# Gate products in the other ring of result banks, norms' sums in the second tile behind, adaLN products out of the query tiles

## The chip, the core and the metric

The kernel runs on one core of one Trainium2 chip. The metric is the device time of one execution in microseconds, taken as the median of several runs. The kernel before takes 1669.76 us (three runs, 1668.8 to 1671.15). Its profile is one further execution.

Five engines work side by side, each through its own instructions in a fixed order, and they wait for each other by semaphores: TensorE (PE, matrix products), VectorE (DVE), ScalarE (ACT), GpSimd (POOL) and SyncE (SP, which issues the DMA loads). "Bank" below means one of the result banks that TensorE writes and that DVE and ACT read.

## The reference

One layer of a hybrid backbone on 256 latent tokens `x` and 256 context tokens `ctx`, width 2048. What matters here:

```python
sh1, sc1, g1, sh2, sc2, g2 = split(silu(c) @ w_ada + b_ada, 6)     # adaLN
h = rms_norm(x, norm1_w) * (1 + sc1) + sh1                         # and the same for ctx
gq, gk, gv, gr, gaf, gab, dq, dk, dv = split(h @ w_in, IN_OFFSETS)
la = log_sigmoid(ga @ w_a_up + b_a) / 16                           # gates of the linear attention
o  = gla_scan(gq, gk, gv, la)                                      # forward and backward, 8 heads
q, k = rope(rms_norm(dq)), rope(rms_norm(dk))                      # per head, width 64
od = (softmax(q0 k0) - lam * softmax(q1 k1)) @ dv                  # differential attention
mix = (sigmoid(..) * (ya @ w_proj_gla) + sigmoid(..) * (yb @ w_proj_diff)) @ w_out
x = x + g1 * mix;  x = x + g2 * conv_ffn(modulated(x))
```

Everything is float32 in and out. The products with weights are made of two rounded halves of each weight (a high half and a low half).

## The kernel before, in words

**Tiles.** Each weight product is a "tile": 128 output columns for all tokens. A tile's weights come in two loads of 512 KB (`fetch`, L233), each split into halves: ACT casts the high half (`whi`, L212), DVE subtracts it to get the low half (`wlo`, L219). Four raw buffers and three buffers of each half go round. The products read them: `col_tile` (L281, L283: latent tokens, lines for `gq`, `gr`, `dq` and the gates) makes 32 products of two lengths for a tile, `col_tile2` (L356 to L358: both streams, `gk`, `dk`) makes 48 long ones. `gv_chunk` and `dv_chunk` (L294 to L296) make value rows: a chunk holds four accumulating banks at once and takes eight loads with 24 products each.

**Stages.** After the first sweep come, in program order: two `gv` chunks, the key and query tiles of the linear attention, the `dk` tiles and `gr` tiles, with four calls of `gla_pair` among them (pairs 0 to 3, two heads each), then `dv_chunk(0)`, `dq` tiles 0 to 3, `dv_chunk(1)`, and eight heads of the differential attention between gate tiles; then projections, output product and feed-forward part, which the change does not touch. A scheduler with a time model of its own sets the order of each engine's instructions from the program's; the pairs and the attention heads have a higher priority, so their small products are put among those of the tiles.

**One `gla_pair`.** Two gate products `z` (L825), one for each direction, each into one bank. ACT and DVE make logarithms and running sums of them (`m`, `l`, `bfb`, `rc`). Then decay factors `e` for each of eight groups: POOL subtracts (`away`, L925), ACT takes exponentials (L928), DVE multiplies (`e`, L930). TensorE makes scores `sc` from the factors (L895) in three groups, of 16, 12 and 8 products with turned keys (`kT`) and states (L879) between; DVE's masked copies `at` (L938) empty the score banks. At the end come the outputs `o` (L959, L962) and their norm's sum `oss` (L701).

**Rings.** Banks are handed out in rings: `acc` with four, `aux0` with two and `aux1` with two. `aux_bank(name, j)` picks `aux0` or `aux1`. Score groups take pairs of one bank from each; turned keys, norm sums and `z` come from `aux0`; the outputs take one of each.

**Norms.** At the end of each `dk` and `dq` tile `heads_norm` copies the bank (`nraw`) and squares it (`nsq`) on ACT and puts a closure in the list `later`. That closure splits the squares into two halves (ACT and DVE, `nlo`, L238) and puts a second one in the list `latest`: the sums `hss` (two products, L660 and L661, in a bank of `acc`), the inverse root (ACT, L318 to L322, DVE), and the rotary part (`roped`: DVE shuffle L714, POOL multiplications L715 and L716, DVE sum L717). `flush` runs the closures of a list. The tiles call it halfway: `flush()` ahead of the second load, and `flush(latest)` some products later in the same half. All norm buffers of the `dk` tiles are single; the `dq` tiles use them as two halves in turn.

**adaLN products.** 128 pieces of the adaLN matrix (512 KB each) are multiplied with a broadcast row and summed on DVE (L380, `araw`). `ada_next(n)` adds `n` to a due count; for each whole piece that falls due it issues DVE's product on the older of two buffers (`ada_dot`) and then SP's load of the next into it (L374). The amounts stand at the tiles' calls and, for gate tiles, in `GATE_ADA`.

Of the kernel before, what the change touches and what calls it, by code (L numbers as in the profile page):

```python
# [45 lines left out]
LATE_ADA = {13: 1, 14: 2}  # L46
ROWS_AT = [4, 4, 2, 1]
WARM = 14
GATE_ADA = [0.25] * 4 + [0.5] * 16 + [1] * 12
NRM = [(0, 0)] * 2 + [(j, j + 1) for j in range(12)] + [(12, 14), (14, 16)]  # L50

_VEC = {}
# [100 lines left out]
def layer_kernel(tc, I, out):  # L153
# [3 lines left out]
    with es:  # L157
# [8 lines left out]
        def aux_bank(name, j=0):  # L166
            return ps.tile([P, 512], F32, tag=f"aux{j}", bufs=2, name=name)
# [33 lines left out]
        later, latest = [], []  # L201

        def flush(work=later):
            for step in [work.pop(0) for _ in range(len(work))]:
                step()
# [49 lines left out]
        def col_tile(src, acts, b, orders=None, adas=0):  # L255

            nk = src.shape[1]
            nq = nk // 4
            tied = orders is not None
            orders = orders or [TURN] * (nq - 1) + [ENDED]
            for k0 in range(0, nk, 8):
                kn = min(8, nk - k0)
                if k0:
                    flush()
                raw = fetch(src[:, k0:k0 + kn, :].rearrange("p a b -> p (a b)"), kn * P)
                if k0 and adas:  # L270
                    ada_next(adas)
                whi, wlo = split(raw[:, :kn * P], kn * P)
                for kk in range(0, kn, 4):
                    order = orders[(k0 + kk) // 4]
                    for which in order:
                        j = int(which[1])
                        k = k0 + kk + j
                        sl = slice((kk + j) * P, (kk + j + 1) * P)
                        first, last = k == 0 and which == "h0", k >= nk - 4 and which == order[-1]
                        if which[0] == "h":  # L280
                            i = PE.matmul(b.rearrange("p (a b) -> p a b", a=2), whi[:, sl], acts[k], start=first, stop=last)  # L281
                        else:
                            i = PE.matmul(b[:, T:], wlo[:, sl], acts[k][:, 1, :], start=False, stop=last)  # L283
                        if tied:
                            tie(i)
                    if k0 and not kk:
                        flush(latest)

        def added(dst, b):
            S.copy(dst, b[:, :T])  # L290
# [457 lines left out]
        with tc.tile_pool(name="gla", bufs=1) as pg:  # L748
# [34 lines left out]
            def col_tile2(src, b, adas=0):  # L783

                for k0 in range(0, KT, 8):
                    if k0:
                        flush()
                    raw = fetch(src[:, k0:k0 + 8, :].rearrange("p a b -> p (a b)"), 1024)
                    if k0 and adas:
                        ada_next(adas)  # L790
                    whi, wlo = split(raw, 1024)
                    for kk in range(8):
                        k = k0 + kk
                        both_tile(b, k, whi, wlo, slice(kk * P, (kk + 1) * P), k == 0, k == KT - 1)
                        if k0 and kk == 3:
                            flush(latest)

            def dk_tile(h):
                ada_next(0.5 if h > 3 else 0.75)
# [10 lines left out]
            def gla_pair(p):  # L810
# [9 lines left out]
                S.copy(wa, wr)  # L820
                V.tensor_tensor(wa[64:96], wr[64:96], wa[64:96].bitcast(F32), op=ALU.subtract)
                for d in range(2):
                    z = aux_bank("z")
                    bias = vcol("ba", d * 4 + p)
                    PE.matmul(z, wa[:, d, :], gaT, start=True, stop=True)  # L825
                    l = pg.tile([P, 512], F32, tag="l", name="l")
                    m = pg.tile([P, 512], F32, tag="m", name="m")

                    S.activation(m, z, AF.Relu, scale=-1.0, bias=nba[:, d * 4 + p:d * 4 + p + 1])
                    S.activation(l, z, AF.Abs, bias=bias)  # L830
                    S.activation(l, l, AF.Exp, scale=-1.0)
                    S.activation(l, l, AF.Ln, bias=1.0)
                    V.scalar_tensor_tensor(m, m, -1.0, l, op0=ALU.mult, op1=ALU.subtract)
                    V.memset(rc[:, d, (T - 1) * (1 - d):(T - 1) * (1 - d) + 1], 0.0)
                    if d == 0:
                        for c in range(2):
                            V.tensor_tensor_scan(bfb[:, 0, c * P:(c + 1) * P], onec[:, :P], m[:, c * P:(c + 1) * P],
                                                 0.0, op0=ALU.mult, op1=ALU.add)
                        V.tensor_tensor_scan(rc[:, 0, T - 2::-1], onec[:, :T - 1], m[:, 2 * T - 1:T:-1],
                                             0.0, op0=ALU.mult, op1=ALU.add)  # L840
                    else:
                        V.tensor_tensor_scan(bfb[:, 1, P - 1::-1], onec[:, :P], m[:, P - 1::-1],
                                             0.0, op0=ALU.mult, op1=ALU.add)
                        V.tensor_tensor_scan(bfb[:, 1, T - 1:P - 1:-1], onec[:, :P], m[:, T - 1:P - 1:-1],
                                             0.0, op0=ALU.mult, op1=ALU.add)
                        V.tensor_tensor_scan(rc[:, 1, 1:], onec[:, :T - 1], m[:, T:2 * T - 1],
                                             0.0, op0=ALU.mult, op1=ALU.add)
# [181 lines left out]
        with tc.tile_pool(name="diff", bufs=1) as pd:  # L1029
# [11 lines left out]
            def dv_chunk(j):  # L1041
                banks = [acc_bank("dvb") for _ in range(4)]

                def emptied(t):
                    (V.tensor_copy if t % 2 else S.copy)(dv[:, t, 512 * j:512 * (j + 1)], banks[t])


                turn = [6, 7, 0, 1, 2, 3, 4, 5] if j else list(range(8))
                for q in turn:
                    if q in turn[1:3]:  # L1050
                        flush((later, latest)[turn.index(q) - 1])
                    raw = fetch(I["w_dv"][j, q].rearrange("p a b -> p (a b)"), 1024)
                    both = split(raw, 1024)
                    ws = []
                    for a in range(2):
                        def halves_of(a=a):
                            if j or q > 1:
                                ada_next(0.5 if j else 1)
                            return [w[:, a * 512:(a + 1) * 512] for w in both]
                        ws.append((2 * q + a, halves_of))  # L1060
                    value_rows(banks, ws, 512, 2 * turn[0], 2 * turn[-1] + 1, emptied)
                    if j:
                        nc.gpsimd.dma_start(X4[2 * q][:, 2:, :], A[2 * q + 1])
                        A[2 * q + 1] = X4[2 * q][:, 2:, :]

            def dq_tile(h):
                ada_next(0.5)
                dq[h] = pd.tile([P, T], F32, tag="dq", bufs=4, name="dq")
                b = aux_bank("dq") if h < 2 else acc_bank("dq")
                col_tile(I["w_in"][15 - NGK + h], A, b)  # L1070
# [375 lines left out]
```

## Time and profile before

| What | us |
|---|---|
| median of three runs | 1669.76 |
| profiled execution | 1669.92 |
| its span, first to last instruction | 1668.1 |
| TensorE busy | 1652.1 |
| DVE busy | 1284.1 |
| ACT busy | 901.4 |
| POOL busy | 298.4 |

The profile lists, for each instruction, start, duration and the idle time of its engine just before it, with what ended that idle time. A matrix product of 512 columns stands with some 0.39 us although the next one starts 0.23 us later, since products overlap; so TensorE's work is better read as products per stretch. Profile lines carry the line numbers of the kernel before. A group of equal instructions that follow each other is one row, with its count.

### The profile page before, as it was taken

Reading aid. Unit: us, or ns where it says so; the run is one execution under the profiler, and the core shown is the slowest. Engines: PE = TensorE matmul, PEld = TensorE weight load, DVE = VectorE, ACT = ScalarE, POOL = GpSimd, SP = SyncE. Lnnn points to the kernel's source line nnn. Section 1 sums busy time; section 2 is a strip of 40 time slices with the busy share of each in tenths; the row PEclk is TensorE's granted clock in tenths of the full one; section 3 lists DMA queues with packets and bytes.
Section 4 is the critical chain, followed back from the end, with each engine's and each line's share of the span. In section 5 each row is a group of like instructions: output and inputs, shape, how many; then the busy total and the mean of one; then the engine's idle time right before and its main releaser. Section 6 shows DMA issues by size and latency. Waiting matters only on the chain.

```text
span 1668.1 us, 25627 instructions
## 1 busy us (share of the span) xinstructions
PE 1652.1 (99%) x9476; PEld 1409.8 (85%) x9476; DVE 1284.1 (77%) x2013; ACT 901.4 (54%) x1503; POOL 298.4 (18%) x328
## 2 busy tenths in 40 slices
PE   9999999999999999999999999999999999999998
PEld 6679988887878888888888998888888888888887
DVE  5888977879686887788888897888888888744544
ACT  5235465755446766556655575555555555433332
POOL 0000212212011000002213201221222122684000
PEclk9999999999999999999999999999999999999999
DMA  9997744436565666788887566777777676777764
GB/s 383 408 362 229 240 164 129 152 114 202 189 231 161 191 190 192 225 281 272 265 269 231 174 205 212 239 226 231 241 237 239 227 234 213 208 219 209 218 192 135
DMA packets 111965, 372.74 MB, mean 223 GB/s; under 512 B 14560, under 2 KB 19680, under 8 KB 111840
## 3 DMA queue, kind: packets, MB, share of 16 engines
q1 hardware_dynamic: 102112, 362.51, 66.7%
q0 software_dynamic: 5696, 4.24, 1.0%
q10 hardware_dynamic: 4032, 4.37, 0.8%
q8 instruction: 74, 1.21, 0.3%
q14 instruction: 51, 0.42, 0.1%
HBM read 364.73 MB, written 2.10 MB: 220 GB/s over the span
## 4 chain that ended last, share of the span: by engine, by line
PE 72%; DVE 1%; DMA 0%; issue 0%; ACT 0%; SPq 0%; DVEq 0%
PE down L1397 14%; PE upg L281 9%; PE upv L281 9%; PE gate L281 7%; PE upv L283 5%; PE upg L283 5%; PE mix L281 4%; PE gate L283 3%; PE mix L283 2%; PE pgb L281 2%; PE pga L281 2%; PE dq L281 2%; PE dvb L295 1%; PE dvb L296 1%; PE dvb L294 1%; PE pga L283 1%
## 5 line engine op out<-in xcount | busy, mean ns | idle before, releaser
L212 ACT CAST whi<-wraw 128x1024 fp32r<-128x1024 f32 (+3 forms) x502 | 515.6, 1028 | 465.3 <-PE down L1397 138.8
L219 DVE TENSOR_TENSOR wlo<-wraw,whi 128x1024 fp32r<-128x1024 f32 (+3 forms) x466 | 565.7, 1215 | 235.1 <-ACT whi L212 226.3
L281 PE MATMUL upg<-x,whi 128*128 128x512 f32 x656 | 229.1, 392 | 0.0
L281 PE MATMUL upv<-x,whi 128*128 128x512 f32 x656 | 229.0, 392 | 0.0
L1397 PE MATMUL down<-whi,g 128*128 128x512 f32 x704 | 216.8, 390 | 0.0
L283 PE MATMUL upv<-x,wlo 128*128 128x256 f32 x656 | 183.2, 281 | 0.0
L283 PE MATMUL upg<-x,wlo 128*128 128x256 f32 x656 | 183.0, 281 | 0.0
L281 PE MATMUL gate<-x,whi 128*128 128x512 f32 x512 | 180.8, 399 | 0.0
L380 DVE CUSTOM_DVE_ANT_0 araw<-araw,cb 128x1024 f32<-128x1024 f32 x128 | 163.3, 1280 | 12.7 <-DMA araw<-in_w_ada 12.7
L219 POOL TENSOR_TENSOR wlo<-wraw,whi 128x1024 fp32r<-128x1024 f32 x36 | 86.9, 2414 | 395.4 <-ACT whi L212 395.4
L1397 PEld LDWEIGHTS down<-whi,g 128*128 128x128 f32 x704 | 132.2, 188 | 27.4
L281 PEld LDWEIGHTS upv<-x,whi 128*128 128x128 f32 x656 | 122.5, 187 | 26.3
L281 PEld LDWEIGHTS upg<-x,whi 128*128 128x128 f32 x656 | 122.4, 187 | 26.3
L283 PE MATMUL gate<-x,wlo 128*128 128x256 f32 x512 | 140.6, 284 | 0.0
L1397 PE MATMUL down<-wlo,g 128*128 128x512 f32 x352 | 137.1, 390 | 0.0
L1315 DVE SCALAR_TENSOR_TENSOR C<-C,vec 128x255 f32<-128x255 f32 x88 | 105.8, 1204 | 36.6 <-ACT C L1314 36.6
L283 PEld LDWEIGHTS upg<-x,wlo 128*128 128x128 f32 x656 | 124.3, 189 | 0.5
L283 PEld LDWEIGHTS upv<-x,wlo 128*128 128x128 f32 x656 | 124.3, 189 | 0.5
L281 PEld LDWEIGHTS gate<-x,whi 128*128 128x128 f32 x512 | 94.7, 188 | 22.0 <-issue 2.9
L283 PEld LDWEIGHTS gate<-x,wlo 128*128 128x128 f32 x512 | 96.7, 189 | 3.3 <-issue 0.7
L281 PE MATMUL mix<-x,whi 128*128 128x512 f32 x256 | 87.8, 394 | 0.0
L1397 PEld LDWEIGHTS down<-wlo,g 128*128 128x128 f32 x352 | 66.1, 188 | 13.7
(333 smaller groups left out, 3197.3 us busy)
## 6 DMA issues: line engine op xcount, KB each, us to landing
wraw<-in_w_up SPq DMA_DIRECT2D x164, 512.0 KB, 4.6
araw<-in_w_ada SPq DMA_DIRECT2D x128, 512.0 KB, 5.3
wraw<-in_w_down SPq DMA_DIRECT2D x88, 512.0 KB, 4.0
wraw<-in_w_gate SPq DMA_DIRECT2D x64, 512.0 KB, 4.2
wraw<-in_w_in SPq DMA_DIRECT2D x58, 512.0 KB, 3.8
ada<-in_w_ad SPq DMA_DIRECT2D x52, 512.0 KB, 9.9
wraw<-in_w_proj SPq DMA_DIRECT2D x32, 512.0 KB, 4.8
wraw<-in_w_out SPq DMA_DIRECT2D x32, 512.0 KB, 4.7
```

The lines of the kernel that those rows point to most:

```text
L212: copied[0] = S.copy(hi[:, :n], raw)
L219: i = e.tensor_tensor(lo[:, :n], raw, hi[:, :n].bitcast(F32), op=ALU.subtract)
L281: i = PE.matmul(b.rearrange("p (a b) -> p a b", a=2), whi[:, sl], acts[k], start=first, stop=last)
L283: i = PE.matmul(b[:, T:], wlo[:, sl], acts[k][:, 1, :], start=False, stop=last)
L294: PE.matmul(o, hi[k][:, ts], whi[:, sl], start=first, stop=False)
L295: PE.matmul(o, lo[k][:, ts], whi[:, sl], start=False, stop=False)
L296: return PE.matmul(o, hi[k][:, ts], wlo[:, sl], start=False, stop=last)
L380: i = V.tensor_tensor_reduce(raw, raw, cb[:, q * 1024:(q + 1) * 1024], 1.0, 0.0, op0=ALU.mult, op1=ALU.add, accum_out=ada2[:, j, q:q + 1])
L1315: V.scalar_tensor_tensor(u[:, 1:], b[:, :T - 1], vcol("conv_w", ct), u[:, 1:], op0=ALU.mult, op1=ALU.add)
L1397: i = PE.matmul(banks[h][t][n], g[:, a, ts], w[n][b], start=k == 0 and (a, b) == (1, 0), stop=k == FT - 1 and b == 1)
```

## The change

It has four parts. The gate products `z` take their banks from `aux1`. In the tiles, and in `dv_chunk`, both lists are flushed at one place, ahead of the second load, the list `latest` first: a closure that `flush()` moves on to `latest` is thus run a tile later than before (the sums stand in the second tile behind the normed one). The eight `dq` tiles no longer call `ada_next(0.5)`; in exchange `dv_chunk(1)` calls it with 0.6875 in place of 0.5 (16 calls), and the first four gate tiles with 0.5 in place of 0.25. The number of adaLN products is the same: 4 fewer, 3 more and 1 more.

```diff
-GATE_ADA = [0.25] * 4 + [0.5] * 16 + [1] * 12
+GATE_ADA = [0.5] * 20 + [1] * 12
...
                 if k0:
+                    flush(latest)
                     flush()
...
-                    if k0 and not kk:
-                        flush(latest)
...
                     if k0:
+                        flush(latest)
                         flush()
...
-                        if k0 and kk == 3:
-                            flush(latest)
...
-                    z = aux_bank("z")
+                    z = aux_bank("z", 1)
...
                     if q in turn[1:3]:
-                        flush((later, latest)[turn.index(q) - 1])
+                        flush(latest)
+                        flush()
...
-                                ada_next(0.5 if j else 1)
+                                ada_next(0.6875 if j else 1)
...
             def dq_tile(h):
-                ada_next(0.5)
```

The scheduler makes a new order of it. First place: TensorE at the gate products of pair 1. Before, the first stands behind the key tile 2 (`gk`) and pair 0's second norm sum (`oss`):

```order
L357 MATMUL gk<-x_1219,whi 128x512
L358 MATMUL gk<-x_1219,wlo 128x512
L701 MATMUL oss<-e,ones 128x256
L825 MATMUL z<-gaT,wa 128x512
L281 MATMUL gq<-x_277,whi 128x512
```

Now, at the end of the tile `dk` 1, right behind pair 0's outputs:

```order
L356 MATMUL dk<-x_1219,whi 128x512
L960 MATMUL o<-at,gv 128x256 x4
L823 MATMUL z<-gaT,wa 128x512
L357 MATMUL dk<-x_1219,wlo 128x512
L355 MATMUL gk<-x_277,whi 128x512
```

It has moved ahead by the 48 products of a `gk` tile. The same holds for pairs 2 and 3, and the rest of each pair follows. The first scores of pair 1 now stand in key tile 3 behind 9 of its 48 products (before in query tile 3, behind 7 of its 32), those of pair 2 in `dk` 5 behind 13 (before in `dk` 6, behind 29), and those of pair 3 in `gr` 4 behind 27 (before in `dv_chunk(0)`, behind 55).

Second place: DVE at the second score group of pair 3. Before, in `dv_chunk(0)`, with adaLN products (`ISA araw`) among the factors and masked copies:

```order
L380 ISA araw,ada_77<-araw,cb 128x1024
L380 ISA ada_77 128x1
L930 TENSOR_TENSOR e<-e,qk 128x512
L380 ISA araw,ada_77<-araw,cb 128x1024
L380 ISA ada_77 128x1
L938 COPY_PREDICATED at<-masks,sc 128x2x128 x2
L930 TENSOR_TENSOR e<-e,qk 128x512
L938 COPY_PREDICATED at<-masks,sc 128x2x128 x2
L219 TENSOR_TENSOR wlo<-wraw,whi 128x1024
```

Now, among `gr` tiles:

```order
L928 TENSOR_TENSOR e<-e,qk 128x512 x2
L936 COPY_PREDICATED at<-masks,sc 128x2x128 x3
L290 TENSOR_TENSOR gr_1286<-gr,gr_1286 128x256
L936 COPY_PREDICATED at<-masks,sc 128x2x128
L219 TENSOR_TENSOR wlo<-wraw,whi 128x1024
L928 TENSOR_TENSOR e<-e,qk 128x512
```

No adaLN product stands among them any more. (Line numbers of the changed kernel are smaller by one or two.)

Third place: TensorE at the sums `hss` of the norm of `dq` tile 2. Before, at the end of `dq` 3, ahead of `dv_chunk(1)`:

```order
L283 MATMUL dq<-x_1208,wlo 128x256
L283 MATMUL dq<-x_1219,wlo 128x256
L281 MATMUL dq<-x_1219,whi 128x512
L660 MATMUL hss<-nlo,bones 128x256
L661 MATMUL hss<-nlo,bones 128x256
L294 MATMUL dvb<-whi,x_1068 128x512
L295 MATMUL dvb<-whi,x_1068 128x512
```

Now, at the end of `dv_chunk(1)`, with those of `dq` 3 behind the outputs `o` of head 0:

```order
L293 MATMUL dvb<-whi,x_971 128x512
L659 MATMUL hss<-nlo,bones 128x256
L660 MATMUL hss<-nlo,bones 128x256
L294 MATMUL dvb<-whi,x_971 128x512
L295 MATMUL dvb<-wlo,x_971 128x512
L1123 MATMUL o<-pT,dv 128x256 x4
L659 MATMUL hss<-nlo,bones 128x256
L660 MATMUL hss<-nlo,bones 128x256
L282 MATMUL dq<-x_277,whi 128x512
```

The sums of `dq` 2 have moved behind all but two products of the chunk, since the chunk holds all four banks of `acc` until then.

## The prediction

> **What bounds the kernel now.** I read the page first, then busy time in stretches of 40 us, then what TensorE waited for, then the instructions around each of its gaps.
>
> The page:
>
> ```profile
> span 1668.1 us, 25627 instructions
> PE 1652.1 (99%) x9476; PEld 1409.8 (85%) x9476; DVE 1284.1 (77%) x2013; ACT 901.4 (54%) x1503; POOL 298.4 (18%) x328
> ```
>
> TensorE is busy for all but 16 us. The change adds and removes no product on it, so it can only give back, or add to, idle time of TensorE in the stretches whose order it alters. Busy time by stretch (length, then PE, PEld, DVE, ACT, POOL with their counts, granted clock, DMA share, GB/s):
>
> ```profile
> 320.00:360.00 40.00, 38.79 (x245) 31.88 (x245) 32.04 (x52) 20.79 (x41) 10.56 (x10) 1.00 0.38 121
> 360.00:400.00 40.00, 40.00 (x228) 34.13 (x227) 34.11 (x52) 26.33 (x53) 7.50 (x6) 1.00 0.52 161
> 400.00:440.00 40.00, 36.89 (x206) 29.93 (x206) 30.73 (x51) 13.85 (x29) 4.41 (x3) 1.00 0.67 220
> 440.00:480.00 40.00, 38.33 (x201) 32.54 (x200) 29.85 (x57) 20.63 (x38) 7.79 (x8) 1.00 0.56 180
> 520.00:560.00 40.00, 40.00 (x235) 33.68 (x235) 34.64 (x74) 29.67 (x60) 4.77 (x4) 1.00 0.58 179
> 720.00:760.00 40.00, 39.81 (x230) 34.71 (x229) 31.27 (x47) 22.36 (x36) 0.00 (x0) 1.00 0.85 279
> 1080.00:1120.00 40.00, 40.00 (x232) 35.33 (x232) 33.92 (x47) 23.79 (x37) 8.12 (x4) 1.00 0.69 217
> 1560.00:1600.00 40.00, 40.00 (x179) 33.12 (x178) 18.16 (x15) 15.63 (x15) 0.00 (x0) 1.00 0.64 195
> ```
>
> Between 320 and 480 us TensorE is short of 1.21 + 3.11 + 1.67 = 5.99 us, at a granted clock of 1.00; from 520 on next to nothing is left to give. The last two rows give the length of a product: 40 / 179 = 0.223 us for one of 512 columns, 40 / 232 = 0.172 us where long and short ones alternate as in `gr` and `dq`.
>
> Four gaps make up the 5.99. In each the last thing to arrive is a DVE result. At the second score group of pair 3, in `dv_chunk(0)`:
>
> ```profile
> 405.16 1.21 DVE L380 CUSTOM_DVE_ANT_0 araw<-araw,cb 128x1024 f32<-128x1024 f32 x1
> 406.31 0.76 DVE L938 COPY_PREDICATED at<-masks,sc 128x256 f32<-128x256 uint8 x2
> 406.97 0.68 DVE L930 TENSOR_TENSOR e<-e,qk 128x512 f32<-128x512 f32 x1
> 407.57 0.76 DVE L938 COPY_PREDICATED at<-masks,sc 128x256 f32<-128x256 uint8 x2
> 408.14 1.61 PE L895 MATMUL sc<-e 64*128 64x128 f32 x24 [1.77 <-DVE at L938]
> ```
>
> At the same pair's outputs, where an adaLN product had first waited for its own load:
>
> ```profile
> 429.73 1.23 DVE L380 CUSTOM_DVE_ANT_0 araw<-araw,cb 128x1024 f32<-128x1024 f32 x1 [1.81 <-DMA araw<-in_w_ada]
> 430.88 0.44 DVE L938 COPY_PREDICATED at<-masks,sc 128x256 f32<-128x256 uint8 x1
> 431.37 1.13 PE L962 MATMUL o<-at,gv 128*128 128x256 f32 x4 [1.34 <-DVE at L938]
> ```
>
> At the sums of `dq` 2, where an adaLN product stands ahead of the low half:
>
> ```profile
> 464.49 1.22 DVE L380 CUSTOM_DVE_ANT_0 araw<-araw,cb 128x1024 f32<-128x1024 f32 x1
> 465.63 0.42 DVE L238 TENSOR_TENSOR nlo<-nsq,nlo 128x256 fp32r<-128x256 f32 x1
> 466.11 0.39 PE L660 MATMUL hss<-nlo,bones 128*128 128x256 f32 x1 [1.67 <-DVE nlo L238]
> ```
>
> And at the sums of `dk` 5, which come half a `gr` tile after the squares are split:
>
> ```profile
> 320.48 0.68 DVE L238 TENSOR_TENSOR nlo<-nsq,nhi 128x512 fp32r<-128x512 f32 x1
> 321.30 0.47 PE L660 MATMUL hss<-nlo,bones 128*128 128x512 f32 x1 [1.21 <-DVE nlo L238]
> ```
>
> 1.77 + 1.34 + 1.67 + 1.21 = 5.99: nothing else is to be won here.
>
> **The gate products' bank.** No instruction is added. In `aux0` the gate products of a pair stand behind the norm sums of the pair before; in `aux1` they stand behind its scores and one output, so they come a tile earlier, and every pair with them. Pair 3 leaves `dv_chunk(0)` but for its last four products and its norm sums. The chunk's adaLN products begin with its third load, and in the new DVE order all of pair 3's masked copies come ahead of the first. So the gaps of 1.77 and 1.34 lose their cause: minus 3.11.
>
> What is late next is the second score group at its new places. After the first group ends, two of its three factors wait on the chain of POOL and ACT; pair 2 shows it with no adaLN product between:
>
> ```profile
> 329.99 0.61 PE L895 MATMUL sc<-qk 64*128 64x128 f32 x8
> 334.34 0.73 ACT L928 ACTIVATE e<-away 128x256 f32<-128x256 f32 x2 [0.59 <-POOL away L925]
> 335.10 0.69 DVE L930 TENSOR_TENSOR e<-e,qk 128x512 f32<-128x512 f32 x1 [0.34 <-ACT e L928]
> L925 POOL TENSOR_TENSOR away<-bfb x28: 1032/1422/1922, 169.5 to 415.3; 128x512 f32<-128x512 f32 x28
> ```
>
> That took 335.79 − 330.60 = 5.2 us; summed from pieces it is three ACT pairs, two subtractions on POOL and one multiplication, 3 × 0.73 + 2 × 1.42 + 0.69 = 5.7 us, and 6.7 us with POOL's longest. The new cover is 28 long products for pair 1 (28 × 0.223 = 6.2 us), 26 for pair 2 (5.8 us, with the two sums of a norm and four key turns beside them), and 42 alternating ones for pair 3 (7.2 us). So the three fit by 0.1 to 1.5 us; with POOL's longest two of them wait 0.5 and 0.9 us. Bounds 0 to 1.4 us. I take 0.5, as pair 2's own row is the nearest and lies below the covers.
>
> [...]
>
> Two groups that the old order splits (pair 2's third scores, pair 3's last outputs) stand whole now. No row prices that alone; at most it adds to the gain, and I count nothing.
>
> **The sums in the second tile behind.** Again no instruction is added; two products and the chain behind them come half a tile to a tile later. The squares are split a whole tile ahead of their sums, so the 1.21 at `dk` 5 goes, and with it the risk of such gaps at the other `dk` tiles. What pays is the buffers. Behind the sums the norm takes until POOL has read `nraw`:
>
> ```profile
> 321.61 0.40 PE L661 MATMUL hss<-nhi,bones 128*128 128x512 f32 x1
> 328.46 0.73 POOL L716 TENSOR_TENSOR dk<-nraw,rope 128x256 f32<-128x256 f32 x1 [6.36 <-DVE nraw L332]
> ACT whi L212 <- PE dk L357: 31.5, 8, 6.7
> ```
>
> 329.19 − 321.7 = 7.5 us. The sums now stand in the middle of `dk` 4 to 7, 24 × 0.223 = 5.4 us ahead of the tile's end, where ACT copies the next `nraw` into the same buffer. ACT would wait some 2.1 us there, and behind it in its queue stand a cast of weights, the copy of a `gr` tile and the factors of a pair. The last row is the cover: ACT has itself waited for TensorE to free a high half, 31.5 us in 8 times, 3.9 us each. While that lead is there, 2.1 us cost nothing. If the lead is gone, each tile costs what it waits (first rival).
>
> The sums of `dq` 2 and 3 go to the end of `dv_chunk(1)`. Those of `dq` 3 need the low half, which stands behind the copy of the chunk's last bank on DVE; the outputs `o` of head 0 are ahead of them on TensorE:
>
> ```profile
> 505.84 1.73 PE o L1125 x8
> 511.93 0.69 DVE L1045 COPY dv<-dvb 128x512 f32<-128x512 f32 x1 [0.64 <-PE dvb L296]
> ```
>
> Copy and low half take 0.69 + 0.42 = 1.1 us from the chunk's end, the outputs 1.73 us. It fits by 0.6 us if the copy starts at once; in its row DVE was free 0.64 us before TensorE released it. Were DVE busy instead, with a subtract of 1.2 us begun just before, 0.6 us would be missing, and with the semaphores 0.7. Bounds 0 to 0.7; I take 0.2.
>
> **The adaLN products.** Four of 1.2 us leave the `dq` tiles on DVE. The one at 464.49 goes, and the sums of `dq` 2 are no longer there either: minus 1.67. `dv_chunk(1)` gets three more (11 for 8), the first gate tiles one. Each brings a load of 512 KB on SP, and pairs of them now stand ahead of a weight load, whose issue waits for the second product. The weights have four buffers. As traffic, three loads in some 45 us are 35 GB/s; the stretch from 720 shows 279 GB/s with TensorE short of 0.19 us, more than the 180 to 220 here. On DVE they stand among the first head's exponentials: two more ahead of `pT`, 2.4 us, or 4.3 us with one wait of 1.81 like that at 429.73. But `pT` now comes 68 products of `dv_chunk(1)` behind the scores, 15.2 us, where before it came 56 behind, 12.5 us, without a gap. Bounds 0 to 1.9; I take 0.3 for this and all places not named.
>
> **Sum.** The profiled execution took 1669.92 us, its span 1668.1 and 1.8 around it. 1669.92 − 5.99 + (0.5 + 0.2 + 0.3) = 1664.9. The median of the runs shown lies 0.16 below that execution, so I say 1664.8, 0.30% less than 1669.76. About 0.2%, 3.3 us, is what a measurement of this kernel tells from no change; it lies at 1666.4.
>
> **Rivals.**
>
> *Slower: ACT's wait for `nraw` reaches TensorE.* Place: the ends of `dk` 4 to 7. Price: 4 × 2.1 = 8.4 us, so 1664.8 + 8.4 = 1673.2. It decides when ACT's lead falls below 2.1 us. For it: `dk` and pairs 2 and 3 now share the same stretch, and single buffers. Against it: a lead of 3.9 us, and fewer adaLN products on DVE there than in the chunks. Chance 0.09.
>
> *Half comes back, through POOL.* The second score groups of pairs 1 and 2 meet POOL at its longest, held up by DVE, and the end of `dv_chunk(1)` its bound: 1.4 + 0.7, and 0.9 elsewhere, 3.0 us of new waits in place of 1.0: 1666.8, no change that can be told. For it: covers that fit by 0.1 us; the scheduler places by its own times, and the four gaps are the places where these were too short. Against it: in the old order such covers held at pairs 0, 1 and 2. Chance 0.20. [...]
>
> *`pT` of the first head waits.* The products of DVE doubled in `dv_chunk(1)` cost up to 1.9 us, and 0.7 at the chunk's end: 1664.8 + 2.6 = 1667.4. Against it: 15.2 us of cover. Chance 0.05.
>
> *It does not do what it says.* The pairs keep their delays and the gaps only move with them to the `gr` tiles, whose products are shorter: 1669.8. Against it: adaLN products stand in front of the late result in three of four gaps, and they don't move along. Chance 0.06.
>
> **How the numbers follow.** The forecast has 0.60. Its own range is 1663.8 (no new wait) to 1666.2. With half coming back and the first head's wait, 0.85 of the chance lies up to 1667.4; run to run the time varies by about 1 us either way, so the range is 1662.6 to 1668.4. Faster by over 0.2%: the forecast alone, 0.60. Within 0.2%: 0.20 + 0.05 + 0.06 = 0.31. Slower: 0.09.
>
> **What would show it.** Right: TensorE's waits no longer list `sc` and `o` behind `at`, nor `hss` behind `nlo`; the busy time of the stretches from 320 to 480 us comes to 39.5 or more in each; DVE is idle at times in the second half of `dv_chunk(0)`. Wrong: TensorE waits for `wlo` or `whi` in the `gr` tiles (first rival), `sc` behind `e` at pairs 1 and 2 (second), `pT` behind `pe` (third). The forecast falls if the idle time of TensorE from 200 to 720 us stays above 2.7 us.

## The result, and the profile after

The changed kernel takes 1664.44 us (median of 6 runs, 1664.33 to 1665.01), the kernel before 1669.53 us beside it (1668.8 to 1671.84): ratio 0.9967, 95% interval 0.9956 to 0.9977, so faster by 0.33%. The forecast was 1664.8 us, faster, within 1662.6 to 1668.4. The profiled execution took 1664.44 us.

The page of after, the waits of TensorE that the change could touch, and busy time by stretch (columns as before):

```profile
span 1662.3 us, 25625 instructions
PE 1651.8 (99%) x9476; PEld 1409.4 (85%) x9476; DVE 1281.5 (77%) x2013; ACT 899.9 (54%) x1503; POOL 300.8 (18%) x328
```

```profile
PE gr L284 <- DVE wlo L219: 1.2, 1, 1.2
...
PE sc L893 <- DVE e L928: 0.5, 1, 0.5
```

```profile
320.00:360.00 40.00, 40.00 (x207) 33.37 (x206) 31.41 (x52) 29.71 (x60) 7.86 (x6) 1.00 0.37 117
360.00:400.00 40.00, 38.32 (x264) 32.31 (x263) 33.81 (x55) 20.95 (x43) 10.26 (x8) 1.00 0.48 149
400.00:440.00 40.00, 40.00 (x181) 33.21 (x180) 26.30 (x45) 10.65 (x16) 0.00 (x0) 1.00 0.71 235
440.00:480.00 40.00, 40.00 (x207) 34.11 (x206) 26.97 (x44) 19.16 (x32) 5.77 (x7) 1.00 0.62 197
```

The stretches that were short of 5.99 us are full, but for 360 to 400 us, which was full and is now short of 1.68. That is all the idle time of TensorE between 200 and 720 us. No `sc` or `o` waits behind `at`, and no `hss` behind `nlo`. Of the signs that the prediction named, one failed: the 38.32 us between 360 and 400 us lie below its 39.5.

Both new waits stand where pair 3 now meets the norm of `dk` 7. The timeline of after, all engines, in order of start:

```profile
372.30 1.23 DVE L219 TENSOR_TENSOR wlo<-wraw,whi 128x1024 fp32r<-128x1024 f32 x1
...
373.03 1.39 POOL L923 TENSOR_TENSOR away<-bfb 128x512 f32<-128x512 f32 x1 [1.43 <-ACT e L926]
373.44 1.53 DVE L928 TENSOR_TENSOR e<-e,qk 128x512 f32<-128x512 f32 x1
375.02 1.61 PE L893 MATMUL sc<-e 64*128 64x128 f32 x24 [0.48 <-DVE e L928]
376.03 0.74 DVE L330 SCALAR_TENSOR_TENSOR nraw<-nraw,nwt,hny 128x512 f32<-128x512 f32 x1
...
378.82 1.76 DVE L219 TENSOR_TENSOR wlo<-wraw,whi 128x1024 fp32r<-128x1024 f32 x1
...
380.85 0.92 DVE L936 COPY_PREDICATED at<-masks,sc 128x256 f32<-128x256 uint8 x2
...
382.95 0.37 ACT L947 COPY e<-sc 128x256 f32<-128x256 f32 x1 [4.21 <-DVE at L936]
...
384.12 1.48 POOL L923 TENSOR_TENSOR away<-bfb 128x512 f32<-128x512 f32 x1 [2.36 <-ACT e L926]
384.95 1.73 DVE L219 TENSOR_TENSOR wlo<-wraw,whi 128x1024 fp32r<-128x1024 f32 x1 [0.24 <-ACT whi L212]
386.74 0.39 PE L284 MATMUL gr<-x,wlo 128*128 128x256 f32 x1 [1.20 <-DVE wlo L219]
```

The 0.48 us: `e` takes 1.53 us beside POOL, where it takes 0.68 us alone. The 1.20 us: the norm of `dk` 7 (from 376.03) stands on DVE ahead of the masked copies; ACT waits 4.21 us at the copy of the pair's state for them, and behind that copy in ACT's queue stands the cast whose low half TensorE needs; the low half then takes 1.73 us beside POOL, where it takes 1.22 us alone.

### The profile page after: what moved, and what is told of

Its sections match the earlier page's. It is cut to its first block, busy times and chain, and to the rows that moved or that the text cites. A ratio compares the mean times of both kernels' runs of the same rounds, so it can differ in the third digit from the quotient of the medians.

```text
span 1662.3 us, 25625 instructions
## 1 busy us (share of the span) xinstructions
PE 1651.8 (99%) x9476; PEld 1409.4 (85%) x9476; DVE 1281.5 (77%) x2013; ACT 899.9 (54%) x1503; POOL 300.8 (18%) x328
## 3 DMA queue, kind: packets, MB, share of 16 engines
q8 instruction: 74, 1.21, 0.3%
## 4 chain that ended last, share of the span: by engine, by line
PE 96%; DMA 2%; DVE 1%; ACT 0%; issue 0%; POOL 0%; DVEq 0%; SPq 0%; POOLq 0%
PE down L1395 14%; PE upg L282 9%; PE upv L282 9%; PE gate L282 7%; PE upv L284 5%; PE upg L284 5%; PE sweep L391 4%; PE gate L284 4%; PE mix L282 4%; PE mix L284 2%; PE pga L282 2%; PE dq L282 2%; PE pgb L282 2%; PE dvb L293 2%; PE dvb L295 2%; PE dvb L294 2%
```

## The experiments

The first question was whether the three edits win what the prediction gave to each. The theory: each of the four gaps is the time for which an adaLN product, or a half of a norm, stands on DVE ahead of a late result, and each edit removes its own gaps. The rivals stand with each run.

**The bank alone.**

```diff
-                    z = aux_bank("z")
+                    z = aux_bank("z", 1)
```

> Only the gate products' bank is changed. Pair 3's first and second score groups then stand in gr tiles, its third group and its outputs in dv_chunk(0), and no sum of a norm is moved. My theory, that each of the four gaps is the time for which an adaLN product or a half of a norm stands on DVE ahead of the late result: the gaps of 1.77 and 1.34 us go, those of 1.21 (dk 5's sums) and 1.67 (dq 2's sums) stay, TensorE idle between 200 and 720 us falls from 6.0 to 2.9 to 3.9 us, and the time is 3.1 us below that of the kernel before or up to 1 us less, 1666.4 to 1667.4. The rival, that the gaps are made by the score groups' own chain of POOL, ACT and masked copies and only move along with the pairs: sc waits in the gr tiles as long as it did in dv_chunk(0), idle stays at about 6 us and the time within 1 us of the kernel before.

1674.85 us (1673.91 to 1678.01) beside 1669.32: ratio 1.0038, 1.0026 to 1.0051. Slower by 5.5 us, which neither had. The `sc` and `o` gaps are gone; two new ones stand at the sums of `dk` norms, near 303 and 372 us. The first, in the timeline:

```profile
301.91 1.27 DVE L332 SCALAR_TENSOR_TENSOR oy<-e,oy 128x256 f32<-128x256 f32 x1
...
303.71 2.16 DVE L930 TENSOR_TENSOR e<-e,qk 128x512 f32<-128x512 f32 x2
305.79 0.68 DVE L238 TENSOR_TENSOR nlo<-nsq,nhi 128x512 fp32r<-128x512 f32 x1
306.62 0.77 PE L660 MATMUL hss<-nlo,bones 128*128 128x512 f32 x1 [3.79 <-DVE nlo L238]
```

and in stretches of 4 us (the granted clock is the third number from the end):

```profile
304.00:308.00 4.00, 1.38 (x3) 1.16 (x4) 4.00 (x5) 1.36 (x3) 1.18 (x1) 0.69 0.17 71
308.00:312.00 4.00, 4.00 (x11) 3.09 (x10) 3.96 (x7) 1.80 (x3) 0.00 (x0) 0.50 0.64 194
312.00:316.00 4.00, 4.00 (x25) 3.08 (x25) 0.71 (x3) 0.70 (x1) 1.43 (x2) 0.95 0.20 73
```

A norm of the pair before (`oy`) and the factors `e` of the new pair stand on DVE ahead of `nlo`, the factors drawn out beside POOL (2.16 us for two, where one takes 0.68 us alone), and the sums come half a tile after the split. What doubles the price is the clock: after the gap it is 0.50. The clock falls short of full by 4 × (0.31 + 0.50 + 0.05) / 0.5 = 6.9 us of half clock, of which the first 1.1 us still lie in the gap (the clock falls at 305.54 us). The second gap (2.70 us) is followed by the same. TensorE's idle time from 200 to 720 us is 8.6 us, 2.6 more than before; the rest of the loss goes with the clock, by run too: 1673.91 us at a mean granted clock of 0.998, 1677.57 and 1678.01 at 0.995. So the theory's count of gaps was no count of the time, and the bank needs the other place of the sums to be of use.

**The sums alone.**

```diff
                 if k0:
+                    flush(latest)
                     flush()
...
-                    if k0 and not kk:
-                        flush(latest)
...
-                        flush((later, latest)[turn.index(q) - 1])
+                        flush(latest)
+                        flush()
```

> Only the place of the norms' sums is changed. Pair 3 stays in dv_chunk(0). My theory: 1.77 and 1.34 us stay, as the adaLN products still stand there; 1.21 goes (the squares of dk 5 are split a tile ahead), and 1.67 goes too although the adaLN products stay in the dq tiles, since the sums of dq 2 now come behind dv_chunk(1). Idle from 200 to 720 us falls from 6.0 to about 3.1 us, the time by 2.9 us to 1666.6. By the theory the new wait for wlo in the gr tiles of the changed kernel (1.2 us) does not come here, because there pair 3 and the norm of dk 7 met, and here pair 3 comes later. The rival, that the later sums delay nraw and ACT by themselves: a wait for wlo or whi of 1 us or more in the gr tiles here too, and a time of 1667.6 or above.

1664.32 us (1663.85 to 1665.19), ratio 0.9971, 0.9960 to 0.9982: as much as the whole change. Both `hss` gaps are gone, that of `dq` 2 with the adaLN products still in the `dq` tiles, and no `wlo` waits in `gr`. Of 3.11 us at pair 3, 2.6 are left, by the very cause that the prediction named (a product that waits for its load, with others and `e` behind it):

```profile
400.21 1.23 DVE L379 CUSTOM_DVE_ANT_0 araw<-araw,cb 128x1024 f32<-128x1024 f32 x1 [2.47 <-DMA araw<-in_w_ada]
...
402.81 1.21 DVE L379 CUSTOM_DVE_ANT_0 araw<-araw,cb 128x1024 f32<-128x1024 f32 x1
...
403.95 0.68 DVE L928 TENSOR_TENSOR e<-e,qk 128x512 f32<-128x512 f32 x1
...
406.61 1.61 PE L893 MATMUL sc<-e 64*128 64x128 f32 x24 [2.26 <-DVE e L928]
```

The time lies 2.3 us below the 1666.6 expected. In the profiled runs 0.5 of it is pair 3's shorter waits and 0.5 small waits of before (0.32 and 0.19 us) that are gone. Another part lies in how a gap is counted: from the modelled end of the product ahead, some 0.39 us behind that product's start, though without a gap the next one starts 0.23 us behind it. Before the sums of `dk` 5, for example, a product starts at 319.70 and the next at 321.30 us: 1.60 − 0.23 = 1.37 us are lost, where the gap says 1.21. Counted so, the four gaps of before cost 6.56 us, the two small waits 0.83, and the two waits left here 2.87: 4.5 us of the 5.0.

**The products alone.**

```diff
-GATE_ADA = [0.25] * 4 + [0.5] * 16 + [1] * 12
+GATE_ADA = [0.5] * 20 + [1] * 12
...
-                                ada_next(0.5 if j else 1)
+                                ada_next(0.6875 if j else 1)
...
             def dq_tile(h):
-                ada_next(0.5)
```

> Only the adaLN counts are changed: none in the dq tiles, more in dv_chunk(1) and the first gate tiles. The order is that of the kernel before up to the end of dv_chunk(0). My theory: 1.77, 1.34 and 1.21 us stay; of the 1.67 at dq 2's sums the 1.2 us of the product ahead of the low half go, up to all of it; idle from 200 to 720 us falls to 4.3 to 4.8 us and the time to 1667.9 to 1668.4. The rival, that the adaLN products on DVE as a whole, and not their places, made DVE late: all four gaps get smaller, and the time falls by 3 us or more.

1672.33 us (1670.01 to 1673.6), ratio 1.0018, 1.0009 to 1.0026: 3.0 us slower. The gap at `dq` 2's sums is still there, and one has come at `pT` of the second head:

```profile
463.01 1.22 DVE L380 CUSTOM_DVE_ANT_0 araw<-araw,cb 128x1024 f32<-128x1024 f32 x1
...
464.15 0.42 DVE L238 TENSOR_TENSOR nlo<-nsq,nlo 128x256 fp32r<-128x256 f32 x1
...
464.62 0.38 PE L660 MATMUL hss<-nlo,bones 128*128 128x256 f32 x1 [1.67 <-DVE nlo L238]
...
526.14 1.22 DVE L380 CUSTOM_DVE_ANT_0 araw<-araw,cb 128x1024 f32<-128x1024 f32 x1
...
528.49 0.74 DVE L1115 SCALAR_TENSOR_TENSOR pe<-pe,sm 128x512 f32<-128x512 f32 x1
...
529.28 1.06 PE L1118 MATMUL pT<-ident,pe 128*128 128x128 f32 x4 [2.19 <-DVE pe L1115]
```

```profile
524.00:528.00 4.00, 3.09 (x18) 2.01 (x16) 3.17 (x6) 3.58 (x8) 0.00 (x0) 1.00 0.59 164
528.00:532.00 4.00, 2.72 (x11) 2.53 (x12) 4.00 (x9) 2.16 (x6) 0.00 (x0) 0.67 0.63 229
532.00:536.00 4.00, 4.00 (x23) 2.95 (x21) 3.25 (x11) 3.07 (x7) 1.65 (x2) 0.90 0.42 131
```

The gap at `dq` 2's sums is 1.67 us before and now, because the product ahead of `nlo` is not one of those that the edit takes out. A count along DVE's queue shows it. In the kernel before, twelve products, from the one at 387.59 us to the one at 425.67, are those of `dv_chunk(0)`. The next two, at 429.73 and 446.32, belong to the `dq` tiles. The two after that, at 460.81 and 464.49, are already those of `dv_chunk(1)`; the scheduler has put them ahead of the chunk's matrix products, which begin at 466.4 us. The middle two of these four rows:

```profile
446.32 1.22 DVE L380 CUSTOM_DVE_ANT_0 araw<-araw,cb 128x1024 f32<-128x1024 f32 x1
460.81 1.22 DVE L380 CUSTOM_DVE_ANT_0 araw<-araw,cb 128x1024 f32<-128x1024 f32 x1
```

With the products alone, those at 429.73 and 446.32 are missing and the other two stand at 459.33 and 463.01 us; up to there the rest of the queue is as before, but for one instruction of a norm that stands one place earlier. The gap of 1.34 has gone because the product at 429.73, which stood ahead of pair 3's last masked copy, was one of the two. So the theory falls for the 1.67, whose product the edit doesn't touch, and holds for the 1.34, which I had not given to this edit; the rival (all four smaller) falls. The product at 526.14, ahead of `pe`, is by the same count one of the gate tiles, which the edit has brought forward. The gap of 2.19 us there is followed by 4 × (0.33 + 0.10) / 0.5 = 3.4 us of half clock, 1.7 us lost.

**The products of `dv_chunk(0)` moved, all else as before.**

```diff
-GATE_ADA = [0.25] * 4 + [0.5] * 16 + [1] * 12
+GATE_ADA = [0.625] * 4 + [0.875] * 16 + [1.375] * 12
...
-                            if j or q > 1:
-                                ada_next(0.5 if j else 1)
+                            if j:
+                                ada_next(0.5)
```

> The kernel before with one other edit: the twelve adaLN products of dv_chunk(0) go to the gate tiles, and pair 3 stays in dv_chunk(0). My theory: the gaps of 1.77 and 1.34 us go or fall below 0.5 each, though neither bank nor place is changed, because nothing of 1.2 us stands ahead of the masked copies any more; 1.21 and 1.67 stay; idle from 200 to 720 us is 2.9 to 3.9 us and the time 1666.4 to 1667.4, unless the gate tiles pay for the products with new waits. The rival, that the pair's own chain is late there by itself: sc and o wait behind at for 1 us or more as before, and the time is within 1 us of the kernel before.

1667.19 us (1666.07 to 1668.79), ratio 0.9988, 0.9979 to 0.9997, as the theory has it. Its stretch from 400 us, with pair 3 in it, is full, and the masked copies now wait for TensorE:

```profile
400.00:440.00 40.00, 40.00 (x224) 32.91 (x224) 21.21 (x41) 14.61 (x30) 4.22 (x3) 1.00 0.26 80
```

```profile
406.34 2.72 DVE L938 COPY_PREDICATED at<-masks,sc 128x256 f32<-128x256 uint8 x6 [1.62 <-PE sc L895]
```

So the cause of the 1.77 and 1.34 is shown to be the adaLN products: neither bank nor place had to change for them to go. The run also bears out the count: without those twelve, the queue goes on with two products at 418.65 and 442.85 us and then two at 457.3 and 461.0. The one at 418.65, of a `dq` tile, still stands ahead of pair 3's last four masked copies, but it waits for no load, where the one at 429.73 had waited 1.81 us, and no `o` waits. A product ahead of a late result is thus no gap by itself.

From here the theory is another: the sums' place is the gain, the products add little or nothing to it, and the bank only takes away the wait that the sums leave in `dv_chunk(0)`. Three runs leave out one edit each (their diffs are those above, two at a time).

> Sums and products together, without the bank. My first theory (each part removes its own gaps) has fallen with the single parts; the new one: the sums' place alone is the gain, the products out of the dq tiles add nothing to it, and the bank only takes away the wait in dv_chunk(0) that the sums alone leave. So this kernel is as the sums alone, 1664.3 us (1663.3 to 1665.3), with one wait of sc behind e of 1 to 2.5 us in dv_chunk(0), where adaLN products stand ahead of e on DVE, and no wait of pT. The rival, that the products cost the first head a wait wherever they are moved, as they did alone (pT behind pe 2.2 us): 1666.5 us or more.

1663.61 us (1663.41 to 1664.58), ratio 0.9967, 0.9955 to 0.9980; `sc` waits behind `e` once, 1.6 us, and `pT` not at all. As expected: with the sums moved, the products do no harm to the heads, and `o` waits for no masked copy, as in the run of the products alone.

> Bank and products together, without the sums. New theory: what made the bank alone slower by 5.5 us were two waits of hss behind nlo near 303 and 372 us (3.8 and 2.7 us), each followed by some 5 us at half the granted clock, because pairs and dk norms then share a stretch of DVE and the sums stand half a tile behind the split. Both are still there without the moved sums, so 1673 to 1677 us, with the granted clock below 1 in those two stretches. The rival, that the bank was slower because of the adaLN products of the dq tiles or by chance of that build: 1668 us or less, and no wait of hss above 2 us.

1675.22 us (1674.33 to 1676.71), ratio 1.0036, 1.0024 to 1.0049. Slower, with the same gaps; but the clock followed only one of them, in the profiled run:

```profile
306.57 0.57 PE L660 MATMUL hss<-nlo,bones 128*128 128x512 f32 x1 [3.79 <-DVE nlo L238]
...
373.28 0.47 PE L660 MATMUL hss<-nlo,bones 128*128 128x512 f32 x1 [2.70 <-DVE nlo L238]
```

```profile
308.00:312.00 4.00, 4.00 (x14) 3.20 (x14) 3.96 (x7) 1.55 (x3) 0.00 (x0) 0.72 0.66 192
...
372.00:376.00 4.00, 2.72 (x15) 2.42 (x16) 4.00 (x6) 1.93 (x3) 0.00 (x0) 1.00 0.57 161
```

So that expectation was half right: the gaps belong to the order, the clock behind them to more than the gap's length.

> Bank and sums together, without the products. The order up to the end of dv_chunk(0) is that of the changed kernel. New theory: 1664.4 us (1663.6 to 1665.4), the same as with the products; the wait of 1.67 at dq 2's sums does not come back, since those sums stand behind dv_chunk(1); sc behind e and gr behind wlo wait 1.7 us together as in the changed kernel. The rival, my prediction's own step, that a product of a dq tile ahead of the low half made that wait: 1 to 1.7 us of it come back, at dq's sums or behind dv_chunk(1), and the time is 1665.4 to 1666.1.

1663.95 us (1663.76 to 1665.15), ratio 0.9971, 0.9960 to 0.9982. TensorE's waits are those of the changed kernel, `gr` behind `wlo` 1.2 and `sc` behind `e` 0.5 us; nothing comes back at `dq`. The rival falls.

**The best version tried**: the sums, and the products of `dv_chunk(0)` moved to the gate tiles; bank and `dq` as before.

> The sums' place, and with it the twelve adaLN products of dv_chunk(0) moved to the gate tiles; bank and dq products as in the kernel before. New theory: all four gaps of before go, and neither the wait of 2.3 us that the sums alone leave in dv_chunk(0) nor the 1.7 us of the changed kernel in the gr tiles come; TensorE idle from 200 to 720 us is below 1 us and the time 1662.5 to 1664.0, up to 2 us less than the changed kernel. The rival, that the products moved to the gate tiles make new waits there (0.4 us at s and 0.6 us at pga when they were moved alone): 1664.4 or above.

1662.95 us (1662.02 to 1664.26), ratio 0.9961, 0.9949 to 0.9974. It was run again beside the changed kernel:

> The changed kernel once more, beside the two others of this call on one chip: 1664.4 us (1663.6 to 1665.2), with 1.2 us of wlo in the gr tiles and 0.5 us of sc behind e again, if these waits belong to the order of the program. TensorE's idle time in the first 40 us, which was 3.9 us in the profile of before and 2.9 us in that of the changed kernel, belongs to none of the three edits: it should come out between 2.8 and 3.9 us whatever the kernel.

> The sums' place with the twelve adaLN products of dv_chunk(0) in the gate tiles, once more, to be set beside the changed kernel on one chip: 1663.0 us (1662.2 to 1664.0), 1.0 to 2.0 us less than the changed kernel, as TensorE's waits from 200 to 720 us are 1.7 us there and none here. If the rival holds, that such a difference is no more than the spread of the start, the two medians lie within 0.5 us.

The changed kernel took 1664.32 us (1664.25 to 1664.55), ratio 0.9969, 0.9956 to 0.9981; the other 1662.19 us (1661.91 to 1662.96), ratio 0.9956, 0.9942 to 0.9970: 2.1 us less, and no run of the one reaches the other. The stretch from 360 to 400 us of the changed kernel, and of the other:

```profile
360.00:400.00 40.00, 38.38 (x264) 32.31 (x263) 33.83 (x54) 20.95 (x43) 10.28 (x8) 1.00 0.47 149
```

```profile
360.00:400.00 40.00, 40.00 (x229) 33.99 (x228) 32.59 (x49) 27.02 (x55) 10.43 (x8) 1.00 0.44 145
```

The 1.6 us are the order's, not a chance of one run. TensorE's idle time in the first 40 us came to 3.5 and 3.4 us here, and to 2.9 to 3.9 in the other ten profiles without gaps made on purpose. It was 3.9 us where the record of the full clock begins at 3.95 us of the span (before), and the first 14 products took 4.82 us there; it was 3.0 us where that record begins at 6.53 us (after), with 6.01 us for the same products. That fits slower products which fill the waits; no run sets that moment on purpose.

**Gaps on purpose.** The clock was a suspect of its own, so gaps were made in the changed kernel at eight places of the `upg`/`upv` stage, by doing a low half's subtraction over again, and in a second kernel on 512 columns and fewer times:

```diff
                 i = e.tensor_tensor(lo[:, :n], raw, hi[:, :n].bitcast(F32), op=ALU.subtract)
+                for _ in range(extra):
+                    i = e.tensor_tensor(lo[:, :n], raw, hi[:, :n].bitcast(F32), op=ALU.subtract)
```

> The changed kernel with gaps made on purpose: at eight places of the stage of upg and upv, some 43 us apart, the subtraction that makes a low half is done 5, 6, 7, 8, 9, 10, 11 and 12 times more on DVE, 1.14 us each, with the same result. TensorE waits there by what DVE's lead does not cover. Theory, from the gaps of 3.79, 3.2, 2.7 and 2.2 us in the runs so far: a gap under 1.9 us leaves the granted clock at 1.00; one over 2 us is followed in some cases, and one over 4 us in every case, by some 5 us at half clock, which cost another 2 to 4 us. The rival, that the low clock in those runs had to do with the stretch and its products and not with the gap: no stretch of this kernel falls below 1.00 but the last, whatever the gaps. The time itself is that of the changed kernel plus the sum of gaps and of these losses; it isn't used.

The gaps came out at 8.9 us and more (106.3 us in 8), too long for what I wanted; all eight had a low clock behind them. The gap of 3.2 us that the expectation names stands in no trace; 3.15 us is the idle time of the bank alone from 360 to 400 us, of which one gap is 2.70. The time, one run, was 1791.06 us: 126.7 more than the changed kernel, 20 more than the gaps. Behind the eight gaps the clock is at half for 37 us in all, so 18.5 of these 20 us are lost clock, 2.3 us for each.

> Shorter gaps made on purpose: as in the run before, but the repeated subtraction is of 512 columns (0.6 us) and is done 1, 2, 3, 4, 2, 3, 4 and 5 times more at the eight places, since there the gaps came out at 8.9 us and more. Theory: gaps under 1.9 us leave the granted clock at 1.00, gaps between 2 and 4 us are followed by half clock in some cases and not in others, longer ones in every case. If the threshold is sharp instead, one length parts all gaps with a low clock behind them from all without.

One run, 1688.23 us. Five gaps; three of them, and the stretches with a gap of 1.75, of 4.03 and of 4.07 us:

```profile
1126.07 0.39 PE L289 MATMUL upv<-x,wlo 128*128 128x256 f32 x1 [1.75 <-DVE wlo L224]
1164.28 0.46 PE L289 MATMUL upv<-x,wlo 128*128 128x256 f32 x1 [4.03 <-DVE wlo L224]
...
1311.84 0.58 PE L289 MATMUL upv<-x,wlo 128*128 128x256 f32 x1 [4.07 <-DVE wlo L224]
```

```profile
1120.00:1160.00 40.00, 38.25 (x217) 32.97 (x215) 35.04 (x49) 21.39 (x34) 7.20 (x3) 1.00 0.65 211
1160.00:1200.00 40.00, 35.97 (x199) 31.41 (x198) 29.89 (x45) 20.44 (x31) 7.25 (x3) 0.96 0.60 200
...
1280.00:1320.00 40.00, 35.93 (x192) 31.25 (x191) 28.70 (x42) 19.31 (x30) 7.24 (x4) 0.91 0.55 184
```

Behind gaps of nearly one length the clock was short by 40 × 0.04 = 1.6 us once and by 40 × 0.09 = 3.6 us another time; behind the two of 1.75 it was not short. In this stage no pair and no norm runs: the gap is the cause. No gap between 2 and 4 us came about here, so for those the runs above speak alone.

## Why the prediction was right or wrong

- **What bounds the kernel, and the four gaps**: right. All four went, and 0.5 us of small waits besides. Their price was too small by some 0.6 us: from start to start they cost 6.56 us, not the 5.99 of the idle time.
- **The gate products' bank, "minus 3.11"**: wrong as a step. The gaps' cause, the adaLN products ahead of the late result, is shown by moving those products alone. But the bank alone costs 5.5 us: I priced it with the sums already in their new place and did not say so, nor ask what pairs that come a tile earlier do to the sums of the `dk` norms there. Beside the sums and the products it is worth nothing that can be told: 1663.61 without it, 1664.44 and 1664.32 with it, in three comparisons.
- **The sums, minus 1.21**: right, and too small. This edit alone brings the whole gain (1664.32), as with it both 1.21 and 1.67 go, and 0.5 us of the other two.
- **The adaLN products, minus 1.67**: wrong, and the step that failed is "the one at 464.49 goes". It stays: it is a product of `dv_chunk(1)`, and those that the edit takes out stood at 429.73 and 446.32. The 1.67 went because the sums of `dq` 2 left. What the edit takes by itself is the 1.34, which the prediction gave to the bank. Products moved alone: 3.0 us slower. Left out of the whole: 1663.95.
- **ACT's wait for `nraw` at the ends of `dk` 4 to 7**: right to take nothing. In after ACT waits 0.2 us once for POOL at that copy. It did lose time elsewhere in these norms: at the copies of their results (L990) it waits 10.2 us from 230 to 400 us, in the kernel before 1.5, but neither of TensorE's two waits ends on it.
- **New waits, 1.0 us**: 1.68 came, and not where I had worked it out. Pairs 1 and 2 and the end of `dv_chunk(1)`, 0.7 us together in the sum, wait not at all; pair 3's second group, whose cover I took for the longest, waits 0.48. The 1.20 in `gr` was to be the sign of the first rival; its chain is another (masked copies behind the norm of `dk` 7, ACT behind the copies).
- **`pT`, in the 0.3**: 0 in after. The mechanism is real: with the products alone it waits 2.19 us and costs 3.9 with the clock, at the second head, not the first.
- **POOL's longest subtraction, 1.92 us**: no bound. That row began at 398.03 us beside an adaLN product and ended 0.96 us after it, where the shortest takes 1.03 us; after has rows of up to 2.26 us. With 2.26 the pieces come to 3 × 0.73 + 2 × 2.26 + 0.69 = 7.4 us, more than each of the three covers. Pairs 1 and 2 did not wait all the same; pair 3, with 7.4 us against a cover of 7.2, is the one that waited.
- **The sum**: 1669.92 − 5.99 + 1.68 = 1665.6, against 1664.44 in the profiled run. Two small waits of before are gone (0.32 at 160 to 200 us, 0.19 at 720 to 760). The first 40 us show 0.9 us less idle time, but that is no gain: taken product by product, the 550th begins at 81.71 us before and 0.28 us later in after. Counted from start to start, the six waits of before that are gone come to 7.39 us and the two new ones to 1.92, so 1669.92 − 7.39 + 1.92 = 1664.45; that covers the 0.7 us that the sum is still too high, though the 0.28 us of the start stand against it. So the number came out in part by luck, by terms that were wrong one by one: the forecast of the whole rested on the sums alone.

## What to carry to other kernels

Price each edit of a change against the kernel before as well as in the company of the others: here one edit was worth the whole, and the other two, alone, cost 3 and 5.5 us. Before an edit is credited with taking an instruction out from ahead of a late result, count along the queue whether it is one of those that the edit removes: its place in the timeline doesn't say which stage issued it. To move the reader of the late result further back helped here whatever stood ahead. And a gap of TensorE can cost more than its own length: none up to 1.81 us lowered the clock here, while one of 2.19 us lost 1.7 us more by the clock, and one of 3.79 us 2.9 us more.

## What the runs showed of the hardware

**The clock after a gap.** No gap up to 1.81 us (products alone, pair 3), the two of 1.75 made on purpose among them, left a mark on the granted clock. Those of 2.19 (products alone) and 2.70 (bank alone) were followed by half clock; 2.26 (sums alone) and 2.70 (bank and products) were not; all from 3.79 up were. The half clock lasted some 3.4 us (products alone: 3.4; the gap of 4.03 made on purpose: 1.6 / 0.5 = 3.2) or twice that (bank alone: 6.9; the gap of 4.07: 7.2) behind gaps of up to 4.1 us. In it a long and a short product took 0.64 us together, where they take 0.35 at full clock (behind the gap that ended at 1164.28 us). Counted at half, what lay behind the gap cost 1.7 us on top of the 2.19, and (312.37 − 306.62) / 2 = 2.9 us on top of the 3.79 of the bank alone.

The times at which the clock changed say what the lengths leave open. With the bank alone they were 305.54, 312.37, 373.81 and 380.63 us: 6.83, 61.44 and 6.82 us apart, which is 2, 18 and 2 times 3.41. In the traces of before and after the clock stands at full from 3.95 to 1666.24 us and from 6.53 to 1661.99 us, which is 487 and 485 times 3.413. Cut into stretches of that length, counted from these times, the two gaps of 2.70 us lie differently. That of the bank alone put 2.04 us of idle time into one stretch, and half clock followed; that of bank and products, where the clock had fallen at 306.8 us and come back at 310.2, was parted into 1.07 and 1.63, and none followed:

```profile
370.39:373.81 3.42, 1.37 (x8) 0.92 (x6) 3.42 (x5) 2.04 (x4) 1.54 (x2) 1.00 0.14 24
373.81:377.22 3.41, 2.76 (x8) 2.30 (x9) 3.41 (x5) 1.46 (x3) 0.00 (x0) 0.50 0.56 173
...
368.24:371.65 3.41, 2.34 (x14) 1.78 (x12) 3.41 (x5) 2.57 (x5) 2.16 (x2) 1.00 0.03 11
371.65:375.07 3.42, 1.79 (x9) 1.60 (x10) 3.42 (x5) 1.31 (x3) 0.33 (x1) 1.00 0.49 153
```

The 2.19 us of the products alone (527.09 to 529.28 us) lay in one stretch: the clock fell at 529.4 us, as that stretch ended. In before, the three stretches that hold most of the gaps of 1.77, 1.67 and 1.21 us had 1.42, 1.36 and 1.21 us idle, and the clock stayed at 1.00. So in these traces the end of a gap went with how it lay in the stretches. No run moved a gap across them on purpose.

**DVE beside POOL.** In the trace of after, every one of ten multiplications `e` (128x512, two inputs, L928) that began while POOL's subtraction ran ended 0.55 us after that subtraction, however long it ran (0.68 us alone). Eleven low halves of 1024 columns began beside it or beside POOL's rotary products; nine of them ended 1.08 or 1.09 us after POOL (1.22 us alone), and the other two, begun in the last 0.11 us of POOL's instruction, 1.13 and 1.15. In the rows above: 373.03 + 1.39 = 374.42 and 373.44 + 1.53 = 374.97; 384.12 + 1.48 = 385.60 and 384.95 + 1.73 = 386.68. The other way round, that subtraction ended 0.9 to 1.0 us after the low half, the `e` or the adaLN product that it met (372.30 + 1.23 = 373.53 for a low half, and 374.42), and that low half, begun first, took 1.23 us, as alone. So in these rows the price of a meeting was the rest of the other's instruction, mostly of one; twice the subtraction (237.54 us, 2.26 us long, and 357.40 us, 2.12 us long) ended only after the rest of a low half and a whole adaLN product. A wait of 0.85 us on DVE (1.53 − 0.68) is what TensorE saw as 0.48 at pair 3.
